# Moving eight of the 32 gate projections of a hybrid layer from its last merge to its front, with the tanh kept in DRAM between the two

## The chip, the cores and the metric

The kernel runs on one core of one Trainium2 chip, as one program. The metric is the time of the program on the device in microseconds (us). The profile times the engines one by one: PE (matrix multiplication) with its weight loads (PEld), DVE (vector), ACT (scalar functions), POOL (a second vector engine) and SP, which in this program only issues DMA transfers. ACT issues DMA transfers too. A row that ends in SPq is an issue on SP's queue.

## The reference

Two layers work on 256 context tokens and 256 latent tokens of width 1024. In each, h is the normalised and modulated input; one large projection of h gives the inputs of four token mixers and a gate of 4 x 1024 channels:

```python
h = modulate(rmsnorm(x, p['norm1_g']), mods[0], mods[1])
ua, ub, uatt, us5, ug = split_sections(h @ p['w_in'])
ya = rwkv7_mixer(ua, ...); yb = gla_mixer(ub, ...)
yc = window_attention(uatt, ...); yd = s5_mixer(us5, ...)
merged = 0.0
for i in range(4):
    merged = merged + sigmoid(gates[i]) * (ys[i] @ p['w_branch'][i])   # gates = split(ug, 4)
x = x + mods[2] * (merged @ p['w_out'])
y = hier_moe(modulate(rmsnorm(x, p['norm2_g']), mods[3], mods[4]), p)   # top-1 group, top-2 of 8 experts
x = x + mods[5] * y
mods = split(silu(c) @ p['w_ada'] + p['b_ada'], 6)                      # adaLN
```

The context tokens go the same way with modulations of their own, but in the second layer only as far as the latent tokens need them.

## The kernel before

Layer 0 has all 512 tokens on its output side (`lo = 0`), layer 1 the 256 latent ones (`lo = 256`, `nlo = 512 - lo`). Activations lie with channels on the partitions, and each float32 operand of the large projections is split into a high and a low part: h into `hh` and `hl` (kept all through the front of a layer), a weight block by `gsplit` on ACT (the high part) and POOL (the rest) into two tiles `gs`. `proj` then makes 128 output channels in 24 matmuls, three for each 128 input channels: `hh,gs` and `hl,gs` with the high part, `hh,gs` with the rest. Almost all matmuls are issued in the helper `mm`, so that their line is L270, and they are told apart by the names of output and inputs. A weight block of 512 KB comes through `gload` (L234, tile `g`) on SP's queue, and the buffers go round: the projections have two raw buffers (pool `wp`).

A layer runs in this order: norm and modulation; S5; GLA; the projections of RWKV (`rwkv_in`, 8 blocks of `in_w_in_rwkv`, seven or eight of them beside other stages); attention; the units of RWKV's recurrence (`rwkv_units`; its first products are called `psc`, and its small transfers `ad<-sm` at L510 pass through DRAM on SP's queue). Beside the recurrence, which is a chain of small steps, PE does the merges of the branches GLA, S5 and attention (`merge` with i = 1, 3, 2), each with eight gate projections, eight reads of `w_branch` (tile `wb`) and eight products. When the recurrence has given its output, branch RWKV is merged last (i = 0). There `merge` runs with `pairs`: the products are split too (`yh,bh`, `yl,bh`, `yh,bl` into `pb`), `wb` and the gate tile have two buffers. Then come w_out and the residual (`project`, `tail`) and the MoE, whose expert weights stream in blocks of 1 MB.

The modulations of adaLN are made by `adaln` in blocks of 128 channels: one load of 512 KB (`g<-in_w_ada`), eight matmuls into tile `ada` (the trace counts two for each, so a block has x16 there), and one addition on DVE into `mods`. The blocks that are not needed at once are spread by two helpers: `early(n)` runs n of them through pool `wx`, which has one buffer, and PSUM bank X, and `some(n)` a few between the chunks of a merge. In layer 0, 24 go through `early(NB)` between S5 and GLA and 24 through `some(C2)` in the last merge, three for each chunk, with two buffers (pool `wy`); in layer 1 all 32 left go through `early(32)` ahead of S5.

The instructions of an engine stand in one list, and SP's transfers in another; each list is worked off in order. Which order the lists have is not that of the program's text: a scheduler mixes the stages when the kernel is built, under the limits of the buffers of each pool and bank. So a stage that stands later in the text can begin earlier, and one load that waits for its buffer holds the loads behind it on SP.

Of the kernel before, what the change touches and what calls it, by code (L numbers as in the profile page):

```python
# [9 lines left out]
F32 = mybir.dt.float32  # L10
# [3 lines left out]
AF = mybir.ActivationFunctionType  # L14
# [161 lines left out]
class Net:  # L176
# [1187 lines left out]
    def merge(self, l, i, h, yT, acc, lo, first, pool, between, pairs=None):  # L1364

        nc, io = self.nc, self.io
        nlo = 512 - lo
        if pairs:
            y = self.split(pool, ("yh", "yl"), yT)
        for c in range(8):  # L1370
            wb = pool.tile([128, 2, 128], F32, tag="wb", bufs=1 if pairs == self.pa else 2, name="wb")
            nc.sync.dma_start(wb, io["w_branch"][l, i, :, :, 128 * c:128 * c + 128])
            ps = self.pa()[:, 0:nlo]
            self.proj(ps, io["w_in_gate"][l, 8 * i + c], h, lo)
            between()
            sg = pool.tile([128, nlo], F32, tag="mg", bufs=1 if pairs == self.pa else 2, name="sg")
            self.act(sg, ps, AF.Tanh, scale=0.5)
            pb = (pairs or self.pa)()[:, 0:nlo]
            if pairs:
                w = self.split(pool, ("bh", "bl"), wb, 1 if pairs == self.pa else 2)  # L1380
            for kp in range(2):
                if pairs:
                    self.mm3(pb, [v[:, kp, :] for v in w], [v[:, kp, :] for v in y], kp == 0, kp == 1)
                else:
                    self.mm(pb, wb[:, kp, :], yT[:, kp, :], kp == 0, kp == 1)
            o = acc[c]
            if first:
                self.stt(o, sg, 1.0, pb, OP.add, OP.mult)
            else:
                self.stt(sg, sg, 1.0, pb, OP.add, OP.mult)  # L1390
                self.tt(o, o, sg, OP.add, nc.gpsimd)

    def project(self, t, w, acc, x, bs, lo, pool):

        s = t // 2
        a = 128 * t - lo
        for n in range(2):
            ps = self.pa()
            for k in range(8):
                self.mm(ps, acc[k][:, a:a + 128], w[n][k], k == 0, k == 7)  # L1400
            tm = pool.tile([128, 512], F32, tag="pm", bufs=2, name="pm")
            self.tt(tm, ps, bs[s][:, 512 * n:512 * n + 512], OP.mult)
            xo = x[t][:, 512 * n:512 * n + 512]
            self.tt(xo, xo, tm, OP.add, self.nc.gpsimd if n else None)
# [357 lines left out]
    def layer(self, l, lo):  # L1762
        nc, tc, io = self.nc, self.tc, self.io
# [4 lines left out]
        fs, hs, rs, bs = (ExitStack() for _ in range(4))  # L1768

        def pool(es, name, side="left", bufs=1):  # L1770
            return es.enter_context(tc.tile_pool(name=f"{name}{l}", bufs=bufs, side=side, reuse_waits="tile"))
# [3 lines left out]
        H = pool(hs, "H", "right")  # L1775
        yT = [H.tile([128, 2, 512 - lo], F32, name=f"yT{i}") for i in range(4)]
        h = [H.tile([128, 8, 512], F32R, name=n) for n in ("hh", "hl")]
        rm, p3, p4 = pool(rs, "rm"), pool(bs, "p3"), pool(bs, "p4")
        wx = pool(bs, "wx")

        self.mres = rm.tile([128, 512], F32, name="mres")
        nc.gpsimd.memset(self.mres, 1.0)
        nc.gpsimd.memset(self.mres.rearrange("p (j t) -> p j t", t=64)[:, :, 0:1], 0.0)

# [30 lines left out]
        todo = [(0, j) for j in range(16, 48)] + [(1, j) for j in range(16)] if l == 0 else [(1, j) for j in range(16, 48)]  # L1815
# [5 lines left out]
        NB, C1, C2 = 24, 0, 3  # L1821

        def early(n):
            for _ in range(n):
                a, j = todo.pop(0)
                self.adaln(a, [j], wx, "X")
        early(32 if l else 0)
        self.bt = "B1"
        self.s5(l, h, s5w, yT[3], lo, p3, s5p)
        self.bt = "B0"  # L1830
        early(0 if l else NB)
        with ExitStack() as es:
            self.gla(l, h, yT[1], lo, pool(es, "p2"))
        st = self.rwkv_in(l, h, lo, rm, p4, lambda: None)
        us = ExitStack()
        up = pool(us, "up", "right")
        self.rwkv_first(l, st, up)
# [63 lines left out]
```

## Time and profile before

| | |
|---|---|
| time, median of 3 runs | 2653.89 us (2648.95 to 2660.78) |
| time of the profiled execution | 2654.23 us |
| its span | 2652.4 us |
| mean granted clock of PE | 0.934 of full speed |
| PE busy | 2417.8 us (91%) |
| PEld busy | 1464.8 us (55%) |
| DVE busy | 1156.0 us (44%) |
| POOL busy | 705.8 us (27%) |
| ACT busy | 660.0 us (25%) |
| DMA | 548.25 MB, mean 207 GB/s |

The span is what the profile covers, some 2 us less than the time. Layer 0 fills about the first 1500 us of it and layer 1 the rest. In layer 0 S5 and GLA stand at 57 to 276 us, attention to 361, the recurrence with three merges to 717, the last merge to 792, the MoE from about 900; in layer 1 S5 and GLA stand at 1500 to 1731, attention to 1797, the recurrence with three merges to 2048, the last merge to 2083, the MoE from about 2150.

### The profile page before, as it was taken

What the parts mean: (1) busy time and instruction counts of PE and PEld (TensorE: products, weight loads), DVE (VectorE), ACT (ScalarE), POOL (GpSimd) and SP (SyncE); (2) the same over time, 40 slices, a digit from 0 to 9 for tenths busy, and PEclk for the clock granted to TensorE, in tenths of its full rate; (3) what the DMA queues carried; (4) which work ended last, traced back from release to release, by engine and by line L of the source; (5) the groups of instructions that cost most, each with busy time, mean ns of one, the idle gap of its engine ahead of it and who ended that gap; (6) DMA issues with size and microseconds to landing.
All of it is one profiled execution on the core that took longest, in us unless ns stands there. A gap on an engine that the chain in (4) does not pass through costs nothing. (4 is left out here: it accounts for less than half of the span.)

```text
span 2652.4 us, 42883 instructions
## 1 busy us (share of the span) xinstructions
PE 2417.8 (91%) x17431; PEld 1464.8 (55%) x17431; DVE 1156.0 (44%) x3013; ACT 660.0 (25%) x1163; POOL 705.8 (27%) x601
## 2 busy tenths in 40 slices
PE   5879989999999899999999797998989989999997
PEld 4757756666764444444443576666768644333332
DVE  6586466474214343222222667657573342122212
ACT  2232543222212111111111313343223211111111
POOL 2223411123431033322332323342224311111121
PEclk8887988999999899999999787887989989999999
DMA  6332111123560699788888233312124579999994
GB/s 220 114 113 89 60 38 36 45 60 111 180 236 18 265 391 370 306 319 340 322 316 336 72 129 113 116 65 82 56 81 147 213 316 419 411 394 399 399 402 171
DMA packets 143693, 548.25 MB, mean 207 GB/s; under 512 B 35028, under 2 KB 66132, under 8 KB 93060
## 3 DMA queue, kind: packets, MB, share of 16 engines
q1 hardware_dynamic: 138224, 539.51, 54.0%
q10 hardware_dynamic: 5268, 5.94, 0.7%
q8 instruction: 141, 2.31, 0.3%
q14 instruction: 60, 0.49, 0.1%
HBM read 541.78 MB, written 3.60 MB: 206 GB/s over the span
## 5 line engine op out<-in xcount | busy, mean ns | idle before, releaser
L270 PE MATMUL pa<-hh,gs 128*128 128x512 f32 (+2 forms) x1440 | 439.4, 378 | 12.6 <-ACT sg L273 5.2
L276 POOL TENSOR_TENSOR gs<-g,gs 128x1024 fp32r<-128x1024 f32 (+1 forms) x106 | 255.5, 2414 | 548.5 <-PE pa L270 214.5
L276 POOL TENSOR_TENSOR ta<-ta,mb 128x512 f32<-128x512 f32 x93 | 127.9, 1382 | 835.4 <-ACT ta L273 835.4
L270 PEld LDWEIGHTS pa<-hh,gs 128*128 128x128 f32 (+1 forms) x1440 | 264.7, 197 | 76.8 <-issue 18.4
L270 PE MATMUL pd<-w,hT 128*64 128x512 f32 x1024 | 276.6, 599 | 13.1 <-ACT hT L273 11.9
L270 PE MATMUL pa<-hl,gs 128*128 128x512 f32 (+2 forms) x720 | 263.9, 378 | 0.0
L270 PE MATMUL pgate<-w,xT 128*64 128x512 f32 x1024 | 251.5, 597 | 0.0
L270 PE MATMUL pup<-w,xT 128*64 128x512 f32 x1024 | 249.2, 594 | 0.0
L270 PEld LDWEIGHTS <-h2p 128*128 128x128 bf16 x2304 | 134.8, 99 | 78.0 <-issue 72.5
L273 ACT ACTIVATE gs<-g 128x1024 fp32r<-128x1024 f32 (+1 forms) x106 | 110.5, 1045 | 245.7 <-PE pa L270 172.4
L270 PE MATMUL pg<-oh,h2p 128*128 128x128 bf16 x2304 | 163.2, 223 | 5.9 <-DVE nv L1680 4.2
L270 PEld LDWEIGHTS pd<-w,hT 128*64 128x64 f32 x1024 | 81.5, 136 | 146.7 <-issue 124.6
L270 PEld LDWEIGHTS pa<-hl,gs 128*128 128x128 f32 (+1 forms) x720 | 143.9, 200 | 30.4 <-issue 11.5
L270 PEld LDWEIGHTS pup<-w,xT 128*64 128x64 f32 x1024 | 78.3, 137 | 143.1 <-issue 139.3
L270 PEld LDWEIGHTS pgate<-w,xT 128*64 128x64 f32 x1024 | 74.8, 137 | 139.8 <-issue 129.2
L270 PE MATMUL py<-yp,oT 128*128 128x512 f32 x384 | 133.3, 441 | 10.9 <-ACT ta L273 5.0
L286 DVE SCALAR_TENSOR_TENSOR hd<-hd,pgate 128x512 f32<-128x512 f32 x32 | 22.0, 688 | 246.6 <-ACT hd L273 246.6
L276 POOL TENSOR_TENSOR x<-x,ta 128x512 f32<-128x512 f32 x93 | 121.6, 1315 | 4.9
L270 PE MATMUL pa<-gs,hh 128*128 128x256 f32 x480 | 111.0, 327 | 6.9 <-POOL gs L276 6.7
L276 DVE TENSOR_TENSOR hd<-hd,pup 128x512 f32<-128x512 f32 x32 | 22.0, 688 | 217.9 <-PE pup L270 217.9
L286 DVE SCALAR_TENSOR_TENSOR yp<-pd,ws,yp 128x512 fp32r<-128x512 f32 x64 | 47.8, 746 | 152.6 <-ACT yp L273 152.6
L273 ACT ACTIVATE yp<-pd,ws 128x512 fp32r<-128x512 f32 x64 | 44.1, 688 | 272.9 <-PE pd L270 272.9
(504 smaller groups left out, 3744.7 us busy)
## 6 DMA issues: line engine op xcount, KB each, us to landing
w<-in_w_g SPq DMA_DIRECT2D x128, 1024.0 KB, 8.0
w<-in_w_d SPq DMA_DIRECT2D x128, 1024.0 KB, 10.6
w<-in_w_u SPq DMA_DIRECT2D x128, 1024.0 KB, 8.6
g<-in_w_ada SPq DMA_DIRECT2D x96, 512.0 KB, 3.7
g<-in_w_in_gate SPq DMA_DIRECT2D x64, 512.0 KB, 3.6
g<-in_w_in_rwkv SPq DMA_DIRECT2D x16, 512.0 KB, 3.5
wb<-in_w_branch SPq DMA_DIRECT2D x64, 128.0 KB, 2.7
w<-in_w_out SPq DMA_DIRECT2D x8, 1024.0 KB, 6.2
```

What stands on the lines that cost most here:

```text
L270: self.nc.tensor.matmul(out, lhsT, rhs, start=start, stop=stop, skip_group_check=True)
L273: self.nc.scalar.activation(out, in_, f, **kw)
L276: (eng or self.nc.vector).tensor_tensor(out, a, b, op)
L286: self.nc.vector.scalar_tensor_tensor(out, a, s, b, op0=op0, op1=op1)
```

## The change

The eight gate projections of branch RWKV (i = 0) leave the last merge of both layers. A new function `gates` makes them after GLA's call, with two raw weight buffers of its own (pool `gr`), four split tiles (pool `gg`) and PSUM bank X; the tanh of each goes to a DRAM tile on ACT's queue. In the last merge SP loads it back into the tile `sg`. The calls of `early` stand behind `gates` in both layers. The pools `gr` and `gg` are closed then, and RWKV's pools `rm` and `p4` lie on the right side in the space that they leave.

```diff
@@ merge
             sg = pool.tile([128, nlo], F32, tag="mg", bufs=1 if pairs == self.pa else 2, name="sg")
-            ps = self.pa()[:, 0:nlo]
-            self.proj(ps, io["w_in_gate"][l, 8 * i + c], h, lo)
-            between()
-            self.act(sg, ps, AF.Tanh, scale=0.5)
+            if (i, c) in self.kept:
+                nc.sync.dma_start(sg, self.kept[i, c])
+                between()
+            else:
+                ps = self.pa()[:, 0:nlo]
+                self.proj(ps, io["w_in_gate"][l, 8 * i + c], h, lo)
+                between()
+                self.act(sg, ps, AF.Tanh, scale=0.5)
+    def gates(self, l, todo, h, lo, pool, raw):
+        was = self.ring, self.gp
+        self.ring, self.gp = [raw] * 2, [(pool, n) for n in ("h0", "h1", "r0", "r1")]
+        for i, c in todo:
+            ps = self.bank("X", "px")[:, 0:nlo]
+            self.proj(ps, self.io["w_in_gate"][l, 8 * i + c], h, lo)
+            sg = pool.tile([128, nlo], F32, tag="sg", name="sg")
+            self.act(sg, ps, AF.Tanh, scale=0.5)
+            self.kept[i, c] = self.dr.tile([128, nlo], F32, name=f"sg{l}_{i}_{c}")
+            nc.scalar.dma_start(self.kept[i, c], sg)
+        self.ring, self.gp = was
@@ layer
-        rm, p3, p4 = pool(rs, "rm"), pool(bs, "p3"), pool(bs, "p4")
+        rz, p3 = pool(rs, "rz"), pool(bs, "p3")
         wx = pool(bs, "wx")
+        gs = ExitStack()
+        graw, gpool = pool(gs, "gr", "right", 2), pool(gs, "gg", "right")
+        self.kept = {}
...
-        early(32 if l else 0)
         self.bt = "B1"
         self.s5(l, h, s5w, yT[3], lo, p3, s5p)
         self.bt = "B0"
-        early(0 if l else NB)
         with ExitStack() as es:
             self.gla(l, h, yT[1], lo, pool(es, "p2"))
-        st = self.rwkv_in(l, h, lo, rm, p4, lambda: None)
+        self.gates(l, [(0, c) for c in range(8)], h, lo, gpool, graw)
+        early(32 if l else NB)
+        gs.close()
+        rm = pool(rs, "rm", "right")
+        with ExitStack() as es:
+            st = self.rwkv_in(l, h, lo, rm, pool(es, "p4", "right"), lambda: None)
```

On SP's queue the change shows best in layer 1, at the end of attention, where the first small transfers of the recurrence (`ad<-sm`) stand. In the kernel before:

```order
L234 DMA g<-in_w_in_rwkv 128x1024
L234 DMA g<-in_w_ada 128x1024 x2
L234 DMA g<-in_w_in_attn 128x1024
L234 DMA g<-in_w_ada 128x1024
L234 DMA g<-in_w_in_attn 128x1024
L234 DMA g<-in_w_ada 128x1024
L234 DMA g<-in_w_in_attn 128x1024 x2
L234 DMA g<-in_w_in_gate 128x1024 x2
L510 DMA ad<-sm 32x4x32 x2
```

And in the changed one, the same place on the same queue:

```order
L234 DMA g<-in_w_in_attn 128x1024
L234 DMA g<-in_w_ada 128x1024 x2
L234 DMA g<-in_w_in_gate 128x1024
L234 DMA g<-in_w_ada 128x1024
L234 DMA g<-in_w_in_gate 128x1024
L234 DMA g<-in_w_ada 128x1024 x19
L1372 DMA wb<-in_w_branch 128x2x128 x3
L234 DMA g<-in_w_in_gate 128x1024 x2
L510 DMA ad<-sm 32x4x32 x4
```

Nineteen adaLN loads in a row now stand ahead of the recurrence's transfers; before, the last adaLN loads stood among those of attention.

On PE, in the changed kernel, the same place in layer 1 (`pa<-hh,gs` and `pa<-hl,gs` are projections of 256 columns, `psc` the recurrence's first products, `yT,wb` a product of the first merge):

```order
L270 MATMUL pa<-hh,gs 128x256
L270 MATMUL pa<-hl,gs 128x256
L270 MATMUL ada<-g,cT 32x128 x96
L270 MATMUL pa<-yT_12369,wb 128x256 x2
L270 MATMUL psc<-ar_15543,bk 128x192 x4
L270 MATMUL pa<-hh,gs 128x256 x5
L270 MATMUL psc<-ar_15543,bk 128x192 x4
```

Twelve adaLN blocks of eight matmuls stand there in one piece, where before no adaLN matmul was left behind attention.

In the last merge of layer 0, PE's list has before, around the sixth chunk of products (`pb`):

```order
L270 MATMUL pa<-hh,gs 128x512 x8
L270 MATMUL ada<-g,cT 32x128 x16
L270 MATMUL pb<-yh,bh 128x512
L270 MATMUL pb<-yl,bh 128x512
L270 MATMUL pb<-yh,bl 128x512
L270 MATMUL pb<-yh,bh 128x512
L270 MATMUL pb<-yl,bh 128x512
L270 MATMUL pb<-yh,bl 128x512
L270 MATMUL pa<-hh,gs 128x512
```

And after:

```order
L270 MATMUL ada<-g,cT 32x128 x16
L270 MATMUL pb<-yh,bh 128x512
L270 MATMUL pb<-yl,bh 128x512
L270 MATMUL pb<-yh,bl 128x512
L270 MATMUL pb<-yh,bh 128x512
L270 MATMUL pb<-yl,bh 128x512
L270 MATMUL pb<-yh,bl 128x512
L270 MATMUL ada<-g,cT 32x128 x16
```

The 24 matmuls of a gate projection between two chunks are gone, and adaLN blocks and products follow each other directly.

## Rows read from the trace of the kernel before

**Rows 1.** Windows: start:end, length, PE, PEld, DVE, ACT, POOL busy, PE clock, DMA share, GB/s
```profile
57.00:276.00 219.00, 196.04 (x1740) 152.27 (x1739) 139.90 (x336) 65.63 (x102) 63.78 (x80) 0.87 0.30 96
200.00:250.00 50.00, 48.26 (x506) 36.34 (x509) 28.18 (x71) 16.13 (x27) 19.30 (x33) 0.72 0.23 73
276.00:361.00 85.00, 79.28 (x483) 57.83 (x483) 50.09 (x135) 43.68 (x106) 29.10 (x29) 1.00 0.16 47
718.00:792.00 74.00, 69.02 (x556) 51.42 (x547) 18.41 (x38) 16.92 (x25) 31.01 (x16) 1.00 0.73 250
1500.00:1731.00 231.00, 203.10 (x1806) 162.15 (x1806) 156.08 (x415) 72.20 (x120) 74.33 (x79) 0.82 0.35 113
1731.00:1797.00 66.00, 60.99 (x354) 43.00 (x351) 36.95 (x91) 30.04 (x67) 23.22 (x30) 0.90 0.15 49
2048.00:2083.00 35.00, 29.83 (x237) 28.56 (x236) 15.33 (x17) 13.46 (x24) 25.58 (x16) 1.00 0.76 271
2150.00:2640.00 490.00, 466.15 (x2492) 186.24 (x2488) 115.11 (x210) 76.22 (x125) 81.35 (x62) 1.00 0.93 380
```

**Rows 2.** Largest PE waits, 57:276 and 1506:1731: us in total, times, longest
```profile
PE pb L270 <- DVE ba L276: 10.3, 5, 3.3
...
PE pc L759 <- POOL ke L276: 8.9, 1, 8.9
```

**Rows 3.** PE timeline: start, length, line, operation, count; both projection widths
```profile
778.84 1.98 PE L270 MATMUL pa<-hh,gs 128*128 128x512 f32 x8
780.75 1.08 PE L270 MATMUL ada<-g,cT 128*32 128x128 f32 x32
...
1721.98 0.28 PE L270 MATMUL pa<-hl,gs 128*128 128x256 f32 x1
...
1723.78 0.28 PE L270 MATMUL pa<-hh,gs 128*128 128x256 f32 x1
```

**Rows 4.** Timeline: two adaLN links, layer 1, matmuls and loads
```profile
1579.54 0.65 PE L270 MATMUL ada<-g,cT 128*32 128x128 f32 x16
1580.25 4.74 SPq L234 DMA_DIRECT2D g<-in_w_ada  x2
...
1583.96 0.65 PE L270 MATMUL ada<-g,cT 128*32 128x128 f32 x16 [0.18 <-DMA g<-in_w_ada]
...
1725.29 0.64 PE L270 MATMUL ada<-g,cT 128*32 128x128 f32 x16
1726.00 0.33 SPq L234 DMA_DIRECT2D g<-in_w_ada  x1
...
1730.44 0.64 PE L270 MATMUL ada<-g,cT 128*32 128x128 f32 x16 [0.66 <-DMA g<-in_w_ada]
```

**Rows 5.** Page, DMA issues: count, KB each, median us to landing
```profile
g<-in_w_ada SPq DMA_DIRECT2D x96, 512.0 KB, 3.7
...
wb<-in_w_branch SPq DMA_DIRECT2D x64, 128.0 KB, 2.7
```

**Rows 6.** PE timeline: edges of the last merge in either layer
```profile
717.48 0.86 PE L270 MATMUL ada<-g,cT 128*32 128x128 f32 x22
...
792.23 2.13 PE L270 MATMUL bs<-mods,cst 128*128 128x512 f32 x4
...
2046.82 1.03 PE L270 MATMUL pa<-yT,wb 128*128 128x256 f32 x4
...
2083.16 0.28 PE L270 MATMUL pb<-yh,bl 128*128 128x256 f32 x1
```

**Rows 7.** SP timeline: eleven adaLN loads in the last merge, layer 0
```profile
760.37 30.37 SPq L234 DMA_DIRECT2D g<-in_w_ada  x11
```

**Rows 8.** PE and SP timelines, layer 1: S5's last product, first ad
```profile
1715.70 1.07 PE L270 MATMUL pb<-m,ug 128*32 128x128 f32 x16
...
1792.00 0.82 SPq L510 DMA_DIRECT2D ad<-sm  x2
...
1797.99 0.97 SPq L510 DMA_DIRECT2D ad<-sm  x2
```

More of the change, by code (lines that the diff above doesn't have):

```diff
@@ L1391, in merge @@
                 self.tt(o, o, sg, OP.add, nc.gpsimd)
+    def gates(self, l, todo, h, lo, pool, raw):
+        nc = self.nc
+        nlo = 512 - lo
+        was = self.ring, self.gp
[8 more added lines that the diff above has]
+        self.ring, self.gp = was
     def project(self, t, w, acc, x, bs, lo, pool):
@@ L1777, in layer @@
         h = [H.tile([128, 8, 512], F32R, name=n) for n in ("hh", "hl")]
-        rm, p3, p4 = pool(rs, "rm"), pool(bs, "p3"), pool(bs, "p4")
+        rz, p3 = pool(rs, "rz"), pool(bs, "p3")
         wx = pool(bs, "wx")
-        self.mres = rm.tile([128, 512], F32, name="mres")
+        gs = ExitStack()
+        graw, gpool = pool(gs, "gr", "right", 2), pool(gs, "gg", "right")
+        self.kept = {}
+        self.mres = rz.tile([128, 512], F32, name="mres")
         nc.gpsimd.memset(self.mres, 1.0)
```

## The prediction

> **What bounds the kernel now.** I read the stage windows first, since the share of busy time over the whole span mixes stages that have different limits. In every stage that the change touches PE is busy almost throughout [rows 1]: 196.0 of 219 us in the S5/GLA stretch of layer 0, 79.3 of 85 in the attention stretch behind it, 69.0 of 74 in the last merge; in layer 1 203.1 of 231, 61.0 of 66, and 29.8 of 35. The MoE of layer 1 is held by PE (466 of 490 us) and by DMA (0.93) together; its first block needs the routing, so whatever its front gains or loses moves the end by as much. So PE work that only changes its place is worth nothing; a gain must come from idle PE time at the new place, and a loss from new waiting. Next I read what PE waits for in the S5/GLA stretches: results of DVE and POOL, in a few long pieces [rows 2]. Those holes (23 us in layer 0, 28 in layer 1) are all that the eight projections can fill. Last I followed one adaLN block (512 KB of w_ada, eight small matmuls, which the trace counts as 16) from its DMA to its matmuls, because the order of the instructions shows that the change moves all of these blocks out of S5/GLA, and they have one buffer (pool wx).
>
> **What moves, layer 0.** One gate projection is 24 matmuls. Eight matmuls take 1.91 us from the start of their group to the next one's [rows 3], so a projection takes 24 x 0.239 = 5.7 us at full clock and eight take 46 us. In the new order only four of them and one rwkv_in projection stand before GLA's last piece, where before some 4.8 of rwkv_in's projections and 24 adaLN blocks of 0.65 us [rows 4] stood. That is 5 x 5.7 = 29 us of filling for 27 + 16 = 43, so S5/GLA may end up to 14 us earlier; since its holes wait for DVE, I take 8 (0 to 14). Behind it, ahead of the units' recurrence, stand four gate projections (23 us), 3.8 more rwkv projections (22) and the 24 blocks (16): 61 us more. Net 53 us (47 to 61).
>
> The adaLN chain comes on top. With one buffer the next DMA is issued when the previous block's matmuls are done (0.71 us after they start), and the next matmuls start 3.7 to 4.4 us after the issue: a link from matmul to matmul is 4.42 us in one pair of rows and 5.15 in another [rows 4]; the median landing time on the page is 3.7 us for 96 such loads [rows 5]. I take 4.75. The Trainium skill's "DMA: Bandwidth & Descriptors" (Anatomy of one DMA) puts a transfer at about 2.0 us plus its bytes over 436 GB/s, a fit for GpSimd's path; by that 512 KB would land in 3.2 us and a link would take 3.9. The rows, of SP's path, show no link as short, and go into the sum.
>
> In layer 0, 23 links of 4.75 us are 109 us. Behind the eighth gate PE has the attention stretch with its 3.2 rwkv projections (85 us), about three more of them (18) and the blocks (16): 119 us. Chain and work are nearly equal, but share SP's queue, on which a load that waits for its buffer holds those behind it; I add 2 us (0 to 10). The recurrence of layer 0 then starts 55 us later (47 to 71). It and the merges of branches 1 and 3 beside it are the same as before.
>
> **Last merge, layer 0.** It lasts from 717.5 to 792.2 us, 74.7 us, and was 8 x 5.7 = 46 us of projections, 24 adaLN blocks and 8 small products [rows 6]. Without the projections the 24 blocks stay, on two buffers, and in PE order all but two of them come after the merge of branch 2. Their eleven last issues took 30.4 us before, ten intervals of 3.0 us with PE work between [rows 7]; half of the single-buffer link is 2.2 us as a lower end. Between them now lie eight gate reads (256 KB) and w_out's four MB. I take 2.6: 21 intervals, 55 us, plus 2 for the first. About 10 us of the first project tile now lie between the blocks. That is 47 us for 74.7: 28 us back (18 to 38), not 46. Layer 0 ends 55 - 28 = 27 us later (9 to 53).
>
> **Layer 1, front.** A projection has 256 columns: 15 matmuls start in 1.80 us [rows 3], 0.12 us each, 2.9 us for 24 at full clock (5.6 if each took twice that, 0.23). All eight stand inside S5/GLA, in place of three of rwkv_in's projections (14 us) and 28 adaLN blocks (18): 23 us for 32, so that stretch is not longer. The adaLN blocks now begin where S5's last quarter multiplies m (1715.7 us before, [rows 8]). Of the 32, 20 stand between six rwkv projections (four of 512 columns, two of 256, 29 us), attention (50 of the 66 us) and themselves (20 x 0.65, 13 us): 92 us of work against 20 links, 95 us. Then twelve stand on PE with nothing between, and on SP 19 in a row, and behind them on both queues are the recurrence's first products (psc) and its first DMAs (ad<-sm). Twelve links are 57 us in which PE has 8 us of work. So the last block is done at 1716 + 95 + 57 = 1868, and the first sub's ad transfers leave by 1873. Before they left at 1792 to 1799 [rows 8]. The recurrence of layer 1 starts 74 us later (links of 4.4 us: 65; of 5.15: 87; S5/GLA shorter or longer by 12 us: 53 to 99).
>
> **Layer 1, last merge.** 2047.9 to 2083.2 us is 35 us [rows 6] with 8 x 2.9 = 23 us of projections. What is left is 8 small products (0.7 us each), splits and additions, and per chunk a wb and a gate read of 128 KB in two buffers; wb lands in 2.7 us [rows 5], so some 2.2 us a chunk. 18 us for 35: 17 us back (10 to 25). Layer 1 ends 74 - 17 = 57 us later (35 to 85).
>
> **Small terms.** The sixteen tanh stores leave on ACT's queue behind the next projection. No row shows a store of this size; the loads of 128 KB (2.7 us) and of 512 KB (3.7) bound it, and a projection of 5.7 us hides either. In layer 1 a store of 2.7 us with issue and tanh is 0.5 us above 2.9, at most 4 us in all. At nothing; if not hidden, 4 us. The four gate weights less in flight during the merges free DMA that nobody waits for.
>
> **Sum.** 2654.2 + 27 + 57 = 2738, against the profiled execution's own 2654.2 us, which lies at the median of the runs (2653.9).
>
> **Rivals.**
> *The clock rises.* At S5/GLA the mean granted clock is 0.87 and 0.82 [rows 1]. PE runs at 1.2 or 2.4 GHz, so 26% and 36% of these stretches, 57 and 83 us, ran at 1.2. If gate projections kept PE at 2.4, up to half of that, 28 + 42 = 70 us, would come back: 2668 us, at the edge of no measurable change. Against it: from 200 to 250 us PE was busy 48.3 of 50 and the clock was 0.72, and the gates replace projections of the same kind. The Trainium skill's "TensorE: Matmul & The Clock Gate" (Part 1) says that the default clock is the slow one and that sustained activity releases it, which speaks for this change by denser work; by the rows density in S5/GLA hardly changes, and the wait of twelve blocks makes a new hole.
> *The blocks hide, and it is faster.* If the adaLN chain ended before attention does and the gates filled the holes, layer 0's 46 us would meet 23 + 6 us of idle, leaving 17, less the 28 from the merge; in layer 1 23 us fit into 28 of idle and 17 come back. 2654 - 11 - 17 = 2626 us. It decides at a link of 92/31 = 3.0 us; no row has less than 4.4.
> *A part of it.* S5's own small DMAs (m<-kd) no longer queue behind adaLN loads on SP, and S5/GLA gets some 25 us shorter per layer: 2688 us. PE's waits there name DVE and POOL, not DMA [rows 2].
> *Longer still.* Links of over 5.2 us, and S5/GLA longer by the gates: above 2792.
>
> **How the numbers follow.** A measurement here tells about 0.5% (13 us) from no change. Forecast (2654 + 9 + 35 = 2698 to 2654 + 53 + 85 = 2792) 0.75; the smaller loss, 2667 to 2698, 0.10; over 2792, 0.05; no change by the clock, 0.05; faster 0.05. So slower 0.90, same 0.05, faster 0.05. The range is the forecast's, a little lower at both ends since a smaller loss is likelier than a larger: 2685 to 2785.
>
> **What would show it.** In the profile after: w_ada loads at one per 4.4 to 5.2 us in a stretch of 19 on SP in layer 1 with PE nearly idle for some 50 us, waiting on DMA of g; the first ad<-sm of layer 1 70 us later against S5's end; eight px projections inside S5/GLA; a last merge of about 47 us in layer 0, paced by w_ada, and of about 18 in layer 1. The prediction is wrong if the twelve blocks run without gaps, if S5/GLA gets shorter by tens of us, or if the last merge of layer 0 loses its whole 46 us.

## The result and the profile after

The changed kernel takes 2743.84 us (median of 4 runs, 2743.07 to 2754.19) against 2652.35 us before on the same chip (4 runs, 2648.95 to 2660.78): a ratio of 1.0349, 95% interval 1.0314 to 1.0384. It is slower by 91 us. The profiled execution has a span of 2741.2 us, 88.8 more than before, at a mean granted clock of 0.922.

Four rows of PE's timeline cut each kernel into the prediction's terms: the last product of the attention branch's merge (there the last merge begins; in layer 1 its last row of four) and the first matmul of the MoE (`pgate<-w,xT`), in either layer. Before they start at 717.2, 901.4, 2046.8 and 2145.8 us; after at 762.5, 926.5, 2156.1 and 2234.8. The MoE of layer 1 moves as a whole: its last `pgate` is 88.7 us late, its first 89.0. The table gives how late each kernel is against the profiled execution of before; layer 1 is counted from layer 0's MoE on, and the sum is taken at the last `pgate` of layer 1. Each row is one execution, those of e2, e15 and e16 the fastest of their kernels (9, 6 and 11 us below the median), so differences of under some 10 us between rows mean little.

| kernel | layer 0, last merge begins | layer 0, MoE begins | layer 1, last merge begins | layer 1, MoE begins | sum by the profile |
|---|---|---|---|---|---|
| predicted | +55 | +27 | +74 | +57 | +84 |
| changed | +45 | +25 | +84 | +64 | +89 |
| e1, blocks at their old calls | +79 | +61 | +46 | +25 | +86 |
| e2, wx with two buffers | +48 | +26 | +25 | +5 | +31 |
| e3, only the blocks moved | +2 | +2 | +47 | +48 | +50 |
| e16, as e3, layer 1 with two buffers | +4 | +3 | -2 | -2 | 0 |
| e4, wy with four buffers | +43 | +12 | +87 | +67 | +78 |
| e5, e2 and e4 together | +52 | +22 | +40 | +18 | +40 |
| e7, as e1, gates in bank A | +37 | +21 | +15 | -7 | +14 |
| e8, layer 1 alone, wx with two | 0 | +2 | +31 | +10 | +13 |
| e12, as e2, four gates in layer 0 | +35 | +20 | +23 | +2 | +22 |
| e11, layer 1 alone, as e7 | -3 | +4 | +12 | -9 | -6 |
| e15, as e11, wy with three | -5 | -9 | +14 | -8 | -17 |
| e17, before, wy with three | -1 | -7 | -3 | -2 | -10 |

The windows of the changed kernel, as in [rows 1]: layer 0's S5 and GLA, the chain's stretch behind it, the last merge; layer 1's S5 and GLA, the chain's stretch, its last 52 us alone and the 51 us behind them, the last merge.

```profile
57.00:276.00 219.00, 199.96 (x1437) 159.56 (x1436) 137.50 (x328) 66.77 (x104) 68.82 (x78) 0.85 0.19 57
290.00:408.00 118.00, 106.00 (x861) 74.85 (x859) 47.98 (x147) 45.17 (x100) 38.43 (x46) 0.99 0.44 148
762.00:835.00 73.00, 54.28 (x477) 27.21 (x476) 20.70 (x47) 6.30 (x13) 12.48 (x11) 0.88 0.85 284
1525.00:1732.00 207.00, 181.65 (x1401) 156.33 (x1401) 151.18 (x374) 68.97 (x114) 76.57 (x76) 0.81 0.21 64
1732.00:1888.00 156.00, 103.08 (x959) 74.38 (x962) 44.88 (x120) 43.25 (x86) 34.05 (x40) 0.83 0.43 138
1836.40:1888.70 52.30, 12.42 (x195) 7.49 (x193) 3.21 (x11) 0.00 (x0) 0.00 (x0) 0.54 0.37 116
1888.70:1940.00 51.30, 40.06 (x168) 29.15 (x164) 36.95 (x103) 16.06 (x32) 18.88 (x18) 0.67 0.29 81
2156.00:2183.00 27.00, 21.17 (x77) 12.68 (x76) 9.17 (x20) 5.31 (x12) 7.29 (x10) 0.87 0.71 229
```

The new hole is the sixth row: 52.3 us of layer 1 in which PE is busy for 12.4, ACT and POOL do nothing, and DVE has 3.2. It is not in S5 and GLA, where PE is as dense as before (182 of 207 us; 203 of 231 in [rows 1]) and the clock no higher (0.85 and 0.81; 0.87 and 0.82 before). That stretch ends earlier: in layer 0 GLA's last products (`pb<-rs,cst`) start at 256.4 us (268.0 before), and in layer 1 S5's last product starts at 1723.55 (1715.70 before [rows 8]), 17 us earlier once the 25 us of layer 0 are taken off.

The whole way to the last merge, in the same form: layer 0 from 57 us on, before and changed; layer 1 from the last `pgate` of layer 0 on, before, changed, e2 and e7.

```profile
57.00:717.16 660.16, 608.55 (x5001) 445.76 (x4999) 367.61 (x991) 208.82 (x386) 181.65 (x156) 0.91 0.26 80
57.00:762.52 705.52, 650.29 (x5167) 482.55 (x5167) 371.96 (x1011) 217.67 (x400) 196.25 (x172) 0.92 0.24 74
1458.10:2046.80 588.70, 521.30 (x4850) 403.42 (x4847) 358.12 (x1060) 192.91 (x356) 188.91 (x181) 0.86 0.30 94
1483.50:2156.05 672.55, 551.38 (x5043) 433.56 (x5040) 368.11 (x1060) 201.88 (x371) 203.58 (x189) 0.84 0.29 90
1484.20:2098.30 614.10, 536.49 (x5042) 419.92 (x5039) 365.30 (x1060) 201.33 (x371) 204.50 (x189) 0.89 0.32 98
1479.20:2082.95 603.75, 533.80 (x5042) 422.58 (x5039) 357.64 (x1060) 202.40 (x371) 210.28 (x189) 0.89 0.32 100
```

In layer 0 the 45 us are 42 us of PE work and 4 of idle time; in layer 1 the 84 us are 54 us of idle time and 30 of PE work.

What PE waits for in layer 1 from 1530 to 1900 us, in total, times and longest; before, the largest wait there was 8.9 us [rows 2], and adaLN loads had 2.9:

```profile
PE ada L270 <- DMA g<-in_w_ada: 45.9, 18, 3.8
PE pb L270 <- DVE ba L276: 10.5, 6, 5.9
```

The chain itself, on PE's timeline of the changed kernel. It begins right behind the eighth gate projection (`px`), and ends in twelve blocks with nothing between:

```profile
1730.92 1.12 PE L270 MATMUL px<-hh,gs 128*128 128x256 f32 x8
...
1732.61 0.64 PE L270 MATMUL ada<-g,cT 128*32 128x128 f32 x16
...
1836.46 0.64 PE L270 MATMUL ada<-g,cT 128*32 128x128 f32 x16
1840.67 0.95 PE L270 MATMUL ada<-g,cT 128*32 128x128 f32 x16 [3.56 <-DMA g<-in_w_ada]
...
1887.67 1.08 PE L270 MATMUL ada<-g,cT 128*32 128x128 f32 x16 [3.75 <-DMA g<-in_w_ada]
1888.69 2.08 PE L270 MATMUL pa<-yT,wb 128*128 128x256 f32 x4
```

And SP's timeline at the same place, where the first `ad<-sm` stood at 1792.00 us before [rows 8]:

```profile
1799.23 85.08 SPq L234 DMA_DIRECT2D g<-in_w_ada  x19
1884.35 6.98 SPq L1372 DMA_DIRECT2D wb<-in_w_branch  x3
...
1900.72 1.76 SPq L510 DMA_DIRECT2D ad<-sm  x4
```

32 blocks from 1732.61 to 1887.67 us are 31 links of 5.00 us; the eleven bare links are 51.21 us, 4.66 each, of which the block waits 3.6 to 3.8 us for its load. Nineteen loads hold SP's queue for 85 us.

The last merge of layer 0 in the changed kernel (PE's timeline), which answers to the first two rows of [rows 6]:

```profile
762.84 1.08 PE L270 MATMUL ada<-g,cT 128*32 128x128 f32 x32
767.19 0.64 PE L270 MATMUL ada<-g,cT 128*32 128x128 f32 x16 [3.27 <-DMA g<-in_w_ada]
...
808.70 3.75 PE L270 MATMUL pa<-w,acc 128*128 128x512 f32 x4 [2.11 <-DMA w<-in_w_out]
...
835.32 1.88 PE L270 MATMUL bs<-mods,cst 128*128 128x512 f32 x4
```

It waits for adaLN loads, and once for w_out, whose loads left SP's queue from 654.9 us on before, ahead of the merge, and now from 800.5.

### The profile page after: what moved, and what is told of

It is laid out like the page before. It is cut to its first block, busy times and chain, and to the rows that moved or that the text cites. A ratio compares the mean times of both kernels' runs of the same rounds, so it can differ in the third digit from the quotient of the medians.

```text
span 2741.2 us, 42976 instructions
## 1 busy us (share of the span) xinstructions
PE 2432.1 (89%) x17431; PEld 1474.1 (54%) x17431; DVE 1159.8 (42%) x3013; ACT 655.1 (24%) x1160; POOL 696.6 (25%) x601
## 5 line engine op out<-in xcount | busy, mean ns | idle before, releaser
L270 PE MATMUL pa<-hh,gs 128*128 128x512 f32 (+2 forms) x1184 | 363.7, 379 | 6.4 <-ACT sg L273 3.1
L270 PEld LDWEIGHTS pa<-hh,gs 128*128 128x128 f32 (+1 forms) x1184 | 217.5, 197 | 61.2 <-issue 16.9
L270 PE MATMUL pa<-hl,gs 128*128 128x512 f32 (+2 forms) x592 | 220.3, 382 | 0.0
L270 PE MATMUL ada<-g,cT 128*32 128x128 f32 x1536 | 73.8, 321 | 88.2 <-DMA g<-in_w_ada 86.6
L270 PEld LDWEIGHTS pa<-hl,gs 128*128 128x128 f32 (+1 forms) x592 | 118.8, 201 | 25.7 <-issue 9.6
```

Of the source, the lines that this page charges most:

```text
L270: self.nc.tensor.matmul(out, lhsT, rhs, start=start, stop=stop, skip_group_check=True)
```

## The experiments

Theories. **Chain** (the prediction's): layer 1's loss is the adaLN chain on one buffer that the change put between GLA and the recurrence. **Moved work**: the projections put ahead of the recurrence cost their time, wherever the blocks stand. **Clock**: PE's clock in S5, GLA or behind the hole makes the difference. Times of before are those of the runs beside each kernel.

**e1, blocks back at their old calls.**

```diff
+        early(32 if l else 0)
         self.bt = "B1"
         self.s5(l, h, s5w, yT[3], lo, p3, s5p)
         self.bt = "B0"
+        early(0 if l else NB)
...
         self.gates(l, [(0, c) for c in range(8)], h, lo, gpool, graw)
-        early(32 if l else NB)
```

> The changed kernel with the adaLN blocks of pool wx back at their old calls (layer 0 between S5 and GLA, layer 1 ahead of S5); the gate projections stay in front. Chain theory: the loss comes from the adaLN chain of one buffer that was put between GLA and the recurrence. Then layer 1's front, 84 us late in the changed kernel, is 0 to 15 us late, and layer 1 as a whole 5 to 20 us faster than before; layer 0's front stays 20 to 45 us late by the projections put ahead of it, less 20 from the last merge. Sum 2645 us (2620 to 2665). Moved-work theory: the projections themselves hold the recurrence up, and the adaLN blocks are only passengers: layer 1 stays over 50 us late and the time over 2715 us.

Measured 2744.45 us (2741.19 to 2745.25), ratio 1.0346 [1.0329, 1.0363]: no better than the change. The chain theory failed here, as it was put. PE's timeline of layer 0 shows why:

```profile
263.98 1.08 PE L270 MATMUL ada<-g,cT 128*32 128x128 f32 x16
268.84 1.01 PE L270 MATMUL ada<-g,cT 128*32 128x128 f32 x16 [3.78 <-DMA g<-in_w_ada]
273.61 1.08 PE L270 MATMUL ada<-g,cT 128*32 128x128 f32 x16 [3.76 <-DMA g<-in_w_ada]
275.10 0.80 PE L270 MATMUL px<-hh,gs 128*128 128x512 f32 x1 [0.40 <-DVE mods L276]
...
325.74 1.98 PE L270 MATMUL px<-hh,gs 128*128 128x512 f32 x8
```

The first gate projection waits for the addition into `mods` that frees the last adaLN block's PSUM tile: both use bank X, which has one buffer and goes to its users in the order of the calls. So all eight projections run after S5, GLA and the chain, bare, for 52.6 us, and RWKV's remaining projections, whose pools lie in the space that the gates leave, only after them. In layer 1 the same takes from 1787.2 to 1817.8 us. In the change the same bank works the other way round, with the adaLN blocks behind the eighth gate projection: the first block's load leaves SP's queue at 1521.58 us, its matmuls start at 1732.61. e7 tests this reading.

**e2, two buffers in wx**; **e12, the same with four gate projections in layer 0**; **e4, four buffers in wy**; **e5, e2 and e4 together**.

```diff
-        wx = pool(bs, "wx")
+        wx = pool(bs, "wx", bufs=2)                                             # e2, e5, e12
-                wx = pool(es, "wy", bufs=2)
+                wx = pool(es, "wy", bufs=4)                                     # e4, e5
-        self.gates(l, [(0, c) for c in range(8)], h, lo, gpool, graw)
+        self.gates(l, [(0, c) for c in range(8 if l else 4)], h, lo, gpool, graw)   # e12
```

> The changed kernel with two buffers instead of one in pool wx. Chain theory: a link falls from 4.7 to 5.0 us to about 2.5, the twelve bare links at the end of layer 1's attention go, and layer 1's front is 10 to 35 us late instead of 84; layer 0, where projections and chain were nearly equal, keeps most of its 25 us. Sum 2680 us (2655 to 2705). Moved-work theory: within 10 us of the changed kernel, over 2730 us. Clock theory (PE's slow clock behind the holes is the price): the holes go, so also a gain, but the granted clock of layer 1's S5, GLA and attention would rise from that of before.

Measured 2695.03 us (2686.03 to 2702.03), ratio 1.0167 [1.0143, 1.0192]. Layer 1 is 5 us late instead of 64, layer 0 26 instead of 25; by the medians 49 us come back, by the profiles 58. The waits of PE from 1735 to 1821 us, where the chain now lies, and two of its blocks:

```profile
PE ada L270 <- DMA g<-in_w_ada: 5.7, 6, 2.5
```

```profile
1815.75 0.65 PE L270 MATMUL ada<-g,cT 128*32 128x128 f32 x16
1818.31 0.64 PE L270 MATMUL ada<-g,cT 128*32 128x128 f32 x16
```

Waiting for adaLN loads is 5.7 us in place of 45.9. This is the chain theory's case for layer 1; for layer 0 it speaks for moved work, as twice the buffers change nothing there. The clock of the same S5 and GLA is 0.83 (0.82 before), but in the chain's stretch it is 0.98 (0.83 in the changed kernel). To the last merge of layer 1 PE is idle 44 us less than in the changed kernel and busy 15 us less for the same matmuls, so most of the 58 us is the waiting, and up to 15 may be the clock's.

> The changed kernel with two buffers in wx and only four of layer 0's eight gate projections moved; the other four stay in the last merge. Moved-work theory for layer 0: four projections of 5.7 us less stand ahead of the recurrence, so the last merge begins 23 us earlier and gives back 10 us less; layer 0 ends 12 us late (6 to 20) instead of 26, and the whole is 6 to 20 us below the same kernel with eight. If layer 0's price is the adaLN blocks behind GLA instead, halving the projections leaves it at 20 to 30 us late, within 5 us of the kernel with eight.

Measured 2677.05 us (2664.64 to 2691.09), ratio 1.0087 [1.0045, 1.0129], 18 us below e2. With four projections fewer ahead of the recurrence the last merge of layer 0 begins 12 us earlier than in e2 (+35, +48), not 23, and gives back 15 us instead of 22; the layer ends 20 us late instead of 26. The direction is that of moved work, the size half of it; of the 18 us in the medians the profiles show 10, and 3 of these are in layer 1, whose order on PE is the same in both. To the last merge of layer 0 PE is busy 639 us, in e2 649, at a granted clock of 0.90 against 0.93; the slower clock may hide the other half, which no run separates. So e12 bears moved work out no more than roughly.

> The changed kernel with four buffers instead of two for the adaLN blocks in layer 0's last merge (pool wy). If that merge is paced by its adaLN loads, as the prediction says, it gets 6 to 18 us shorter: 2732 us (2725 to 2738). If it is paced by the reads of tanh and w_branch or by w_out, nothing changes: 2743 us (2739 to 2748).

Measured 2731.00 us (2728.57 to 2741.61), ratio 1.0303 [1.0276, 1.0329]. The largest wait of PE in the last merge, in the changed kernel (762 to 836 us) and in e4 (760 to 806), one row each:

```profile
PE ada L270 <- DMA g<-in_w_ada: 14.3, 9, 3.3
```

```profile
PE ada L270 <- DMA g<-in_w_ada: 9.0, 10, 2.4
```

From the beginning of the last merge to the MoE layer 0 gives back 31.5 us, with two buffers 20.2. So the adaLN loads pace the merge: part of what the eight projections leave is taken by waiting for them. Even here 46 us are not reached: SP's queue still carries 24 loads of 512 KB and w_out, at a DMA share of 0.88.

> The changed kernel with two buffers in pool wx and four in layer 0's last merge (pool wy). If the chain of the one buffer (layer 1) and the pace of the adaLN loads in the last merge (layer 0) are two separate prices, their gains add: 12 us below the kernel with wx alone at two buffers, 2675 to 2690 us, and 15 to 30 us above before, which is the moved work of layer 0. If both gains come from one cause, the sum is no lower than with wx alone: 2686 to 2702 us.

Measured 2693.30 us (2677.87 to 2695.87), ratio 1.0116 [1.0067, 1.0165]: by the total not below e2. By stages the gains do add: the merge of layer 0 gives back 30 us (22 in e2). Layer 1, whose order on PE is that of e2, is 13 us longer in this execution, and the windows from its first product to the last merge, of e2 and of e5, show in what:

```profile
1821.00:2098.00 277.00, 253.01 (x2705) 196.17 (x2703) 164.16 (x548) 88.77 (x184) 77.45 (x52) 0.91 0.27 81
```

```profile
1821.00:2108.00 287.00, 263.76 (x2699) 203.88 (x2698) 163.72 (x546) 88.10 (x183) 77.37 (x52) 0.86 0.26 78
```

The same work takes 10 us more at a granted clock of 0.86 instead of 0.91. Executions of one kernel lie up to 26 us apart in e7 and e12, and up to 32 in the kernel before beside e5, so e5's total is inconclusive.

**e3, only the adaLN blocks moved, in the kernel before**; **e16, the same with two buffers in layer 1**.

```diff
-        early(32 if l else 0)
...
-        early(0 if l else NB)
...
+        early(32 if l else NB)
         st = self.rwkv_in(l, h, lo, rm, p4, lambda: None)
-        wx = pool(bs, "wx")
+        wx = pool(bs, "wx", bufs=2 if l else 1)        # e16
```

> The kernel before with only the adaLN blocks of pool wx moved behind GLA; all gate projections stay in the last merge. Chain theory: layer 1's recurrence starts 70 us later (60 to 95), nothing comes back in its last merge, layer 0 ends 10 to 35 us later. Sum 2740 us (2715 to 2775), the whole loss without a single gate projection moved. Moved-work theory: PE has the same work ahead of the recurrence as before, so no change, 2652 us (2640 to 2670).

Measured 2707.32 us (2704.63 to 2714.98), ratio 1.0215 [1.0196, 1.0234]: a loss of 54 us without one gate projection moved (50 by the profile, 48 of them in layer 1), but less than expected. PE's timeline of layer 1:

```profile
1607.48 0.65 PE L270 MATMUL ada<-g,cT 128*32 128x128 f32 x16
...
1800.90 1.08 PE L270 MATMUL ada<-g,cT 128*32 128x128 f32 x16 [3.25 <-DMA g<-in_w_ada]
...
1834.39 1.08 PE L270 MATMUL ada<-g,cT 128*32 128x128 f32 x16 [3.88 <-DMA g<-in_w_ada]
1835.87 1.65 PE L270 MATMUL psc<-ar,bk 64*128 64x192 f32 x4 [0.40 <-DVE mods L276]
```

With bank X free of gates seven blocks run inside S5 and GLA, the first at 1501 us and the others from 1607 us on, and the chain ends at 1834 us. The last row shows one way in which the chain holds the recurrence: the kernel gives `psc` the banks X and C in turn, each with one buffer. Three groups of `psc` run at 1793 to 1798 us; the next waits for the addition into `mods` that frees the last block's tile. No run gave `psc` another bank, so bank X and SP's queue are not told apart here. In layer 0 the blocks end beside attention, and cost 2 us, so the moved blocks alone are not layer 0's price.

> The kernel before with the adaLN blocks of pool wx moved behind GLA, no gate projection moved, and two buffers in wx in layer 1. The move with one buffer cost 50 us in all, 48 of them in layer 1. Chain theory: with two buffers the links of 4.7 us halve, layer 1 is late by 0 to 18 us, and the whole is 2662 us (2650 to 2675). If the place of the blocks costs something else (their order against the recurrence on PE or SP), 30 us or more stay: over 2680 us.

Measured 2665.84 us (2654.45 to 2674.63), ratio 1.0057 [1.0037, 1.0077]; the profiled execution, the fastest of the eight, took 2654.45 us and shows layer 1 2 us early where e3 was 48 late. By the medians 12 us remain that the profile does not show. So moving the blocks costs 54 us with one buffer and 12 with two, by the medians.

**e7, as e1, with the gate projections in bank A**; **e8, the change in layer 1 alone with two buffers**; **e11, e7 in layer 1 alone**; **e15, e11 with three buffers in wy**; **e17, the kernel before with three buffers in wy**.

```diff
-            ps = self.bank("X", "px")[:, 0:nlo]
+            ps = self.pa("px")[:, 0:nlo]                                     # e7, e11, e15
...
-        wx = pool(bs, "wx")
+        wx = pool(bs, "wx", bufs=2 if l else 1)                              # e8
...
+        early(0 if l else NB)                                                # e8, ahead of GLA
...
-        self.gates(l, [(0, c) for c in range(8)], h, lo, gpool, graw)
+        if l:
+            self.gates(l, [(0, c) for c in range(8)], h, lo, gpool, graw)     # e8, e11, e15
+            early(32)                                                        # e8
...
-                wx = pool(es, "wy", bufs=2)
+                wx = pool(es, "wy", bufs=3)                                  # e15, e17
```

> The changed kernel with the adaLN blocks of pool wx at their old calls, as in the first experiment, but with the gate projections in PSUM bank A instead of X. Bank theory: in the first experiment the projections ran without cover only because bank X, with one buffer in the order of the calls, let none of them start before the last adaLN block. In bank A layer 1's eight all stand inside S5 and GLA, so layer 1 is within 12 us of before instead of 25 late; in layer 0 only two of the eight find room there, so it stays 20 to 45 us late. Sum 2685 us (2660 to 2710). Moved-work theory: the projections ahead of the recurrence cost the same wherever they stand, 2744 us (2730 to 2755).

Measured 2667.04 us (2653.41 to 2679.55), ratio 1.0046 [1.0016, 1.0077]: 77 us below e1 for a change of bank. The first and the last rows of `px` in layer 1 (PE's timeline) lie inside S5 and GLA, where e1 had them from 1787 us on:

```profile
1637.25 0.38 PE L270 MATMUL px<-hh,gs 128*128 128x256 f32 x1
...
1729.59 0.50 PE L270 MATMUL px<-hh,gs 128*128 128x256 f32 x2
```

The bank theory holds: layer 1 is 7 us shorter than before, layer 0 still 21 us longer.

> The change in layer 1 alone, with two buffers in wx there; layer 0 keeps its gate projections in the last merge and its adaLN blocks between S5 and GLA. If layer 0's price is the work put ahead of its recurrence and layer 1's the chain, both are gone: layer 1 within 10 us of before, the whole 2657 us (2645 to 2668), no measurable difference. If two buffers only paid off through layer 0's order, layer 1 is late by 30 us or more: over 2680 us.

Measured 2664.61 us (2661.33 to 2672.44), ratio 1.0041 [1.0012, 1.0069]. Layer 0 is 2 us late, layer 1 10: what the last merge gives back (21 us) is less than its front loses (31). The new places of the pools alone cost layer 0 nothing: its last merge begins within 3 us of before here and in e11.

> The change in layer 1 alone, its gate projections in PSUM bank A, and all adaLN blocks at their old calls with one buffer; layer 0 stays as before. By the run with both layers in bank A (layer 1 was 7 us shorter than before there, layer 0 21 us longer) the whole is 2647 us (2638 to 2657), faster by 0.3 per cent or too little to tell. If the gates' gain of 20 us in layer 1's last merge is eaten by the front as in the run with layer 1 alone in bank X, 2664 us.

Measured 2650.88 us (2642.60 to 2657.67) against 2653.31: ratio 0.9993 [0.9976, 1.0010], no difference that can be told.

> The kernel of the run beside this one with three buffers instead of two for the adaLN blocks of layer 0's last merge, whose gate projections are still there. PE is busy 70 of 75 us in that merge before, so at most 5 us can come back: 0 to 5 us below the run beside it. If that merge is paced by the adaLN loads here too, 8 to 13 us below it.

Measured 2644.60 us (2638.66 to 2652.72) against 2653.31: ratio 0.9970 [0.9954, 0.9986], the one kernel here below before, by 0.3%. It is 6 us below e11, a little more than PE's idle time in that merge had allowed.

> The kernel before with three buffers instead of two for the adaLN blocks of layer 0's last merge, and nothing else. If the 6 us that the third buffer brought beside layer 1's moved gates are its own, it is 2647 us (2642 to 2651), and moving layer 1's gates is worth 0 to 5 us. If they came only with the moved pools of layer 0, it is 2653 us (2650 to 2657).

Measured 2648.38 us (2636.95 to 2657.41) against 2649.95 beside it: ratio 0.9984 [0.9966, 1.0002], inconclusive. How much of e15's 9 us is the third buffer's and how much the moved gates' stays open; by the profiles, one of each kernel, the last merge of layer 0 is 10 us shorter in e15 than in e11 and 6 us in e17 than before, and layer 1 is 7 to 9 us shorter in e7, e11 and e15 and 2 us in e17.

## Why the prediction was right

The time (2743.84 us; predicted 2738, 2685 to 2785) and its main mechanism were right: a chain of adaLN loads on one buffer that ends almost bare in front of layer 1's recurrence, and a last merge paced by loads. How close the sum came is in part luck, since errors of 8 to 10 us lie in opposite directions.

**Layer 1, front** (predicted 74, 53 to 99): 84 us. The twelve blocks without cover came as predicted, 51.2 us between the first and the last of them. Counted on top of layer 0's 25 us, the chain began 9 us before the predicted 1716, its covered links were 5.2 us instead of 4.75 (1732.61 to 1836.46, twenty of them), the bare ones 4.66, and the first `ad<-sm` left at 1900.7, that is 1875.5 against a predicted 1873. The 10 us between 74 and 84 lie in the other end: the prediction counted from the last of the `ad` transfers of before (1799), and all of the recurrence moved with the first (1792; 83.5 us late there, 84.1 at the last merge). S5 ended 17 us earlier, where the prediction had that stretch unchanged, so against S5's end the first `ad<-sm` is 101 us later and not 70. Two bounds were also added up wrongly: by its own terms links of 4.4 us give 67 and not 65, and 53 to 99 less 10 to 25 is 28 to 89 and not 35 to 85. The Trainium skill's "DMA: Bandwidth & Descriptors" (Anatomy of one DMA) would give 3.2 us for such a load, an estimate of its fit for GpSimd's path; the page of the profile shows 3.6 us for 96 loads on SP's path, and the link adds the eight matmuls and the issue.

**Layer 1, last merge** (predicted 17 back, 10 to 25): 20 us back to the MoE, and 20 to 22 in every kernel with layer 1's eight projections moved. About half of it shows as project work that has moved in front of the last product.

**Layer 0, front** (predicted 55, 47 to 71): 45 us, just below the bound. The term that was off is the moved work, 53 us net: PE's work to the last merge grew by 42 us. S5 and GLA ended 12 us earlier where 8 were taken; the rest, some 4 us, is open. The chain, nearly as long as the work, added nothing that shows, as predicted within 2 us: e2 with half the chain has the same front (48), and e3 with the blocks alone has 2.

**Layer 0, last merge** (predicted 28 back, 18 to 38): 20 us. The step was right, as e4 shows: adaLN loads pace it. The pace was slower than the 2.6 us taken: in the merge and the first project tile 24 blocks are spread over 71 us (762.84 to 833.78), w_out's loads among them. So layer 0 ends 25 us late for a predicted 27, by two errors of 10 and 8 us that cancel.

**S5 and GLA.** The prediction put layer 1's eight projections (23 us) in the place of 32 us of other work, charged that work only as cover of the chain, and gave the moved projections no price of their own. This is the step that was incomplete: with the chain out of the way they cost time, and nothing of the 28 us of idle time was filled. In e7, whose blocks stand at their old calls, PE's idle time to the last merge of layer 1 is 70 us (67 before) and its work 12 us more, and the front is 15 us late; in e11 it is 12. What goes into one stretch pushes RWKV's projections out of it, and PE work ahead of the recurrence costs its length. In e2, e8 and e12, with two buffers and the blocks behind the gates, the front is 23 to 31 us late, so that order still costs some 8 to 19 us there. Nor did the prediction see that bank X, and not only the place of the calls, puts the whole chain behind the eighth projection (e1, e3, e7).

**Rivals.** The clock did not rise in S5 and GLA. Blocks that hide would have made it faster: e2 and e16 hide them, and e2 is still 1.67% slower, since layer 0 pays for moved work. S5 and GLA did get shorter, by 12 and 17 us; but in layer 1 alone 28 blocks of 0.65 us had left them, so this needs no faster small DMAs, and the time did not come back, as the chain ends last. **Small terms**: the page shows the stores of tanh landing in 2.0 us (256 KB) and 2.2 us (128 KB), well inside a projection in layer 0 and inside 2.9 us in layer 1; the reads take 4.2 us in the crowded queue of layer 0. Keeping tanh on the chip instead was not tried.

```profile
sg<-sg ACTq DMA_DIRECT2D x8, 256.0 KB, 2.0
...
sg<-sg SPq DMA_DIRECT2D x8, 256.0 KB, 4.2
...
sg<-sg ACTq DMA_DIRECT2D x8, 128.0 KB, 2.2
```

## What to carry to other kernels

Before moving work to fill idle time, look at what the move does to everything that shares its queue, its buffers and its PSUM bank: here a chain of small blocks with one buffer, harmless inside a long stretch, became 51 us almost without work once it stood last, and a second buffer took 49 us of the time back. Two users of a bank with one buffer ran in the order of the calls here, and another bank for one of them took back 77 us (e1, e7). And matmul work put ahead of the recurrence cost its length, since the idle time there was waiting for results and not for want of work; what it freed behind the recurrence came back only as far as no transfer took its place.

## What the runs showed that was not expected

The same work differs in time with the clock: layer 1's recurrence took 277 us at a granted clock of 0.91 in e2 and 287 at 0.86 in e5, with PE idle for 24 and 23 us of it. In the hole of the changed kernel, where PE ran sixteen small matmuls per 4.66 us, the clock was 0.54 of full speed, nearly always the lower of its two levels (1.2 and 2.4 GHz), and the same sixteen took 1.08 us instead of 0.64; it stayed at 0.67 for the next 51 us, where the recurrence's start before had 0.78 (1797 to 1848 us). In the 51 us themselves that cost nothing that the stages show, as the recurrence is as late at its end (84.1 us) as at its start (83.5). The Trainium skill's "TensorE: Matmul & The Clock Gate" (Part 1), by which the slow clock is the default and sustained activity releases it, agrees with the row of the hole.
